# A decoder layer on one Trainium2 core: scores of query blocks 4 and 5 in three PSUM banks a head instead of four

## The chip, the cores and the metric

The kernel runs on one core of a Trainium2 chip. Its time is the device time of one execution, in microseconds (us). A core has five engines that run side by side, each through its own list of instructions: TensorE (PE in the profile) multiplies matrices, VectorE (DVE), ScalarE (ACT) and GpSimd (POOL) work on elements, SyncE (SP) issues transfers. TensorE writes its products into PSUM, which has eight banks of 512 float32 columns on each of 128 partitions; VectorE and ScalarE read them there. A bank can be written again only when the last reader of what it held is done.

## The reference: what is computed

One layer of a decoder: 1024 tokens, width 1024, float32. The part that matters here is the sparse attention (8 heads of width 64 in 2 groups of 4, in blocks of 128 queries). For each query block and head it makes three softmaxes: over the selected keys, over a local window of 512 keys, and over 63 compressed keys. With 16 blocks of 64 keys to choose of 16, all keys up to the query are selected.

```
ss = jnp.einsum('qghd,gqkd->qghk', qi, k_sel) * scale     # selected keys
p_s = softmax(where(smask, ss, NEG))
sw = jnp.einsum('qghd,kgd->qghk', qi, k_win) * scale      # local keys
p_w = softmax(where(wmask, sw, NEG))
o = gi[..., 0:1] * o_c + gi[..., 1:2] * o_s + gi[..., 2:3] * o_w
```

Besides there are a retention mixer, projections, gates for both mixers and an MLP.

## The kernel before

Every float32 product is made of three fast products of operands that were split into a high and a low half (in the attention scores, of two). The kernel goes through the layer in stages; the change touches the attention stage alone, which the trace shows from 365 us to about 758 us.

**Units.** The attention stage is cut into 32 units: query blocks 7 down to 0, two key groups, two pairs of heads (line 1093). Unit n has a generator of scores, `scores` (line 962), and one of weighted sums, `pv` (line 1029). A third generator makes the gates of the mixers, `gate_pieces` (line 899), in pieces of eight steps of three matmuls; it has nothing to do with attention and fills TensorE in between.

**Order.** The order of TensorE's instructions is written out by hand (line 113). `place` (line 1097) gives each step of each generator a place on a line of time on which a unit has length 1: the steps of unit n's scores lie evenly between n - 1 + 0.08 and n - 1 + 0.6, so beside the weighted sums of unit n - 1 (constants on lines 41 and 42); the steps of pv of unit n lie between n and n + 1.05; the gates take 8 steps a unit there. `prep_q` (line 948), which transposes the queries of the next group, lies at 0.9 before every second unit. The sorted list is then run step by step. How many steps the scores have, so how far they lie apart, says `n_scores` (line 1082). For the other engines the framework settles the order when the program is built.

**A step of scores.** A step takes a bank of the pool `psS` (four banks, line 937), makes two matmuls in it (tile `S`: high and low half of the queries), and then VectorE reduces each part of it (line 1007: it adds the mask, scales by -1/8 and takes the least value of each row, in place). When all parts of one softmax are reduced, VectorE takes the lesser of the two row values (line 1012), and ScalarE makes the exponentials (line 1016), which read the bank and write `pS` or `pW` in SBUF, with the sum of each row. The exponentials are the last readers of the bank. After the last ones of a head VectorE makes the factor `cf` (lines 1020 to 1023), and GpSimd scales `pS` and `pW` by it (line 1025).

**Banks of blocks 5 and 4.** Block 5 has 768 selected keys and 640 local ones, block 4 640 and 640. So a head has four steps and four banks: 512 selected keys; the other 256 (128) selected ones; 512 local keys; the last 128 local keys with the 64 compressed ones, which lie behind them in the key tile and are multiplied in the same two matmuls. The exponentials of the selected keys come after the second step, those of the local and the compressed keys after the fourth. A unit has two heads, so eight steps.

**A step of pv.** Weighted sums need the transpose of the probabilities. A step either transposes four blocks of 128 x 128 (lines 1060 and 1061) into a bank of the pool `psT` (two banks, line 938; tile `pt`), after which ScalarE copies the high half (`ph`, line 1062) and VectorE the low half (`pl`, line 1063), or it multiplies a pair that is two steps older by the values (tile `O`). The bank of `psT` is free when `pl` is done. `prep_q` takes its bank from the same two (tiles `QQ` on line 954 and `ql` on line 955). In block 5 a unit transposes six times; with T for transposing and M for multiplying the steps are T T T M T M T M T M M, and M again in the next unit.

**The gates' banks.** A piece of the gates holds one bank, of the pool `psO`, or, for odd pieces from number 15 on (line 907), one of `psS` for a whole unit; with four banks in that pool the scores of unit 14 (block 4) have three.

Of the kernel before, what the change touches and what calls it, by code (L numbers as in the profile page):

```python
# [9 lines left out]
F32 = mybir.dt.float32  # L10
F32R = mybir.dt.float32r
I32 = mybir.dt.int32
AF = mybir.ActivationFunctionType
OP = mybir.AluOpType
# [3 lines left out]
P = 128  # L18
S = 1024
# [5 lines left out]
BIGPOS = 3e38  # L25
# [84 lines left out]
def hybrid_block(ctx: ExitStack, tc: tile.TileContext, a: dict, out: bass.AP):  # L110
    nc = tc.nc
    V, A, G, T = nc.vector, nc.scalar, nc.gpsimd, nc.tensor
# [42 lines left out]
    def mm(o, w, m, start, stop):  # L155
        T.matmul(o, w, m, start=start, stop=stop)  # L156
# [60 lines left out]
    with ExitStack() as es:  # L217
# [12 lines left out]
        with ExitStack() as e1:  # L230
# [380 lines left out]
            tail = []  # L611
            for c in range(2):
                for j in range(NT if c else 0):
                    if j == NT - 1:
                        later(1, lambda: rt.update(t=ret_t(0)))
                    ps = psA.tile([P, 512], F32, name="mm", tag="mm")
# [318 lines left out]
    with ExitStack() as e3:  # L935
# [12 lines left out]
        def prep_q(qb, g):  # L948
# [10 lines left out]
                load_q(7 - nxt // 2, nxt % 2)  # L959
            yield  # L960

        def scores(qb, g, hp, u):
            QQ, ql = qs[qb, g]
            nk, nw = qb + 1, min(qb + 1, 5)
            cS, cW = nk * P, nw * P
            w0 = (nk - nw) * P
            u.update(nk=nk, nw=nw, P=[])

            def mask(c0, n, width, edge):
                if c0 + n == width:  # L970
                    return edge_m[:, 640 - n:]
                return edge_m[:, :n] if edge else edge_m[:, P:P + 1].to_broadcast([P, n])

            for i in range(2):
                h = hp * 2 + i
                sums = smp.tile([P, 5], F32, name="sums")
                mx = at.tile([P, 5], F32, name="mx", bufs=4)
                cf = at.tile([P, 3], F32, name="cf", bufs=4)
                pS = at.tile([P, 1024], F32, name="pS", bufs=PS_S)
                pW = at.tile([P, 768], F32, name="pW", bufs=PS_S)  # L980
                G.memset(pW[:, 704:], 0.0)
                for base, KK, start, width, p in ((1, KKs, 0, cS, pS), (2, KKw, w0, cW, pW)):
                    groups = []
                    for c0 in range(0, width, 512):
                        n = min(512, width - c0)
                        groups.append([(base if c0 == 0 else base + 2, KK, start + c0, n,
                                        mask(c0, n, width, base == 2), p[:, c0:c0 + n])])
                    split = len(groups) > 1
                    if base == 2:
                        tail = (0, KKc, 0, 64, cmp_m[:, 56 - 8 * qb:120 - 8 * qb], pW[:, 640:704])  # L990
                        if groups[-1][0][3] <= 448:
                            groups[-1].append(tail)
                        else:
                            groups.append([tail])
                    exps = []
                    for gi, grp in enumerate(groups):
                        ps = psS.tile([P, 512], F32, name="S")
                        off = 0
                        done = []
                        for b, K, c0, n, mk, o in grp:  # L1000
                            done.append((b, ps[:, off:off + n], mk, o))
                            off += n
                        _, K, c0 = grp[0][:3]
                        mm(ps[:, :off], QQ[:, h], K[:, g, c0:c0 + off], True, False)
                        mm(ps[:, :off], ql[:, h], K[:, g, c0:c0 + off], False, True)
                        for b, sc, mk, o in done:
                            V.tensor_tensor_reduce(sc, sc, mk, -0.125, BIGPOS, OP.add, OP.min, mx[:, b:b + 1])  # L1007
                            exps.append((b, sc, o))
                        if gi < len(groups) - 1:
                            yield  # L1010
                    if split:
                        V.tensor_tensor(mx[:, base:base + 1], mx[:, base:base + 1], mx[:, base + 2:base + 3],
                                        op=OP.min)
                    for b, sc, o in exps:
                        m = b - 2 if b > 2 else b
                        A.activation(o, sc, AF.Exp, bias=mx[:, m:m + 1], scale=-1.0, accum_out=sums[:, b:b + 1])  # L1016
                    if base == 1:
                        yield
                if cS > 512:
                    V.tensor_add(sums[:, 1:3], sums[:, 1:3], sums[:, 3:5])  # L1020
                V.reciprocal(cf, sums[:, :3])
                hd = g * 4 + hp * 2 + i
                V.tensor_mul(cf, cf, gts[:, qb, hd * 3:hd * 3 + 3])
                for b, v in ((1, pS[:, :cS]), (2, pW[:, :cW]), (0, pW[:, 640:704])):
                    G.tensor_scalar(v, v, cf[:, b:b + 1], 1.0, op0=OP.mult, op1=OP.mult)  # L1025
                u["P"].append((pS, pW))
                yield
# [53 lines left out]

        def n_scores(qb):
            sel, win = (qb + 4) // 4, (min(qb + 1, 5) + 3) // 4 + (1 if qb == 3 else 0)
            return 2 * (sel + win)

        def n_pv(qb):
            return 2 * ((qb + 1 + min(qb + 1, 5) + 2) // 2)
# [608 lines left out]
```

## Time and profile before

| | |
|---|---|
| time, median of 3 runs | 1570.58 us (1570.36 to 1570.7) |
| the profiled execution's own time | 1570.09 us |
| its span, first to last instruction | 1568.3 us |
| mean granted TensorE clock | 0.999 |
| matmuls shown / instructions | 7845 / 22711 |
| scores of units 8 to 15 (blocks 5 and 4) | about 505 to 606 us |

In the profile a line of the timeline has the start in us, the duration, the engine, the line of the kernel (L1016 is line 1016), the operation, the tiles as output<-inputs, and in brackets the time for which the engine was idle before it with what ended that. L156 is the helper `mm` of all matmuls, so there the tile tells what it is: `S` scores, `O` weighted sums, `gps` gates, `pt` transposes. PEld is the load of the fixed operand, which goes on beside the matmuls. The ends of matmuls are modelled, so the distance from one start to the next says what a matmul costs, not its duration.

### The profile page before, as it was taken

The numbers are of one execution on the slowest core, as the hardware profiler recorded it, in microseconds if no ns is written. First come the engines' busy times: TensorE is split into PE (matmuls) and PEld (weight loads), VectorE is DVE, ScalarE is ACT, GpSimd is POOL, SyncE is SP. The second block draws the span as 40 slices with busy tenths as digits, with TensorE's granted clock in tenths as the row PEclk, the third lists the DMA queues.
The fourth block names the chain that finished last, engine by engine and source line by source line (L and its number), as shares of the span: only waits on it lengthen the run. The fifth ranks groups of instructions, "written<-read, shape, count | busy, mean of one in ns | idle before, by whom it ended". The sixth has DMA issues, their size and how long they took to land.

```text
span 1568.3 us, 22711 instructions
## 1 busy us (share of the span) xinstructions
PE 1544.0 (98%) x7845; PEld 1293.8 (82%) x7845; DVE 1084.4 (69%) x2213; ACT 729.2 (46%) x1633; POOL 418.5 (27%) x496
## 2 busy tenths in 40 slices
PE   9999999999999999999999999999999999999997
PEld 7788888987888888888888888788888888888886
DVE  6875664765777777776755379777777677876673
ACT  5653553754676767676522134222222244443452
POOL 3020010001333323333000001654444446521320
PEclk9999999999999999999999999999999999999999
DMA  6202111342111111121544332544444597664472
GB/s 226 68 18 64 58 32 27 113 150 77 48 35 55 41 42 55 48 61 61 181 155 150 109 119 95 165 168 151 149 156 157 185 379 243 210 211 129 144 272 88
DMA packets 99157, 191.85 MB, mean 122 GB/s; under 512 B 26633, under 2 KB 30097, under 8 KB 99041
## 3 DMA queue, kind: packets, MB, share of 16 engines
q1 hardware_dynamic: 97584, 186.87, 36.2%
q10 hardware_dynamic: 832, 1.64, 0.3%
q0 software_dynamic: 624, 1.88, 0.3%
q8 instruction: 62, 1.02, 0.3%
q14 instruction: 55, 0.44, 0.1%
HBM read 140.02 MB, written 50.33 MB: 121 GB/s over the span
## 4 chain that ended last, share of the span: by engine, by line
PE 86%; DVE 6%; ACT 3%; issue 2%; POOL 1%; POOLq 0%; ACTq 0%; DVEq 0%
PE mmu L156 23%; PE mm L156 20%; PE mmd L156 19%; PE gps L156 9%; PE S L156 4%; PE O L156 3%; PE pt L1061 2%; PE pt L1060 2%; ACT pW L1016 1%; PE pO L156 1%; DVE S L1007 1%; DVE pl L1063 1%; PE pc L156 1%; ACT pS L1016 1%; PE pD L156 0%
## 5 line engine op out<-in xcount | busy, mean ns | idle before, releaser
L1213 DVE TENSOR_TENSOR wl<-raw,wh 128x1024 fp32r<-128x1024 f32 x121 | 185.2, 1556 | 65.5 <-ACT wh L1212 64.0
L1212 ACT ACTIVATE wh<-raw 128x1024 fp32r<-128x1024 f32 x121 | 125.4, 1056 | 207.7 <-PE mmd L156 125.7
L156 PE MATMUL mmd<-wh 128*128 128x512 f32 x448 | 174.3, 389 | 0.0
L156 PE MATMUL mmd<-wl,wh 128*128 128x512 f32 x448 | 174.3, 389 | 0.0
L156 PE MATMUL mmd<-wh,wl 128*128 128x512 f32 x448 | 174.3, 389 | 0.0
L156 PE MATMUL mm<-wh,bh 128*128 128x512 f32 (+1 forms) x416 | 160.8, 390 | 1.6 <-ACT bh L269 1.3
L156 PE MATMUL mm<-wh,bl 128*128 128x512 f32 (+1 forms) x416 | 154.9, 376 | 0.0
L156 PE MATMUL mm<-wl,bh 128*128 128x512 f32 (+1 forms) x416 | 154.3, 375 | 0.0
L1063 DVE TENSOR_TENSOR pl<-pt,ph 128x512 fp32r<-128x512 f32 (+1 forms) x160 | 103.8, 649 | 32.1 <-ACT ph L1062 29.8
L1062 ACT ACTIVATE ph<-pt 128x512 fp32r<-128x512 f32 (+1 forms) x160 | 90.5, 568 | 55.2 <-PE pt L1061 52.8
L1007 DVE CUSTOM_DVE_ANT_0 S<-S,edge_m 128x512 f32<-128x512 f32 (+3 forms) x192 | 100.9, 530 | 16.4 <-PE S L156 14.0
L156 PE MATMUL gps<-bh,wh 128*128 128x512 f32 x256 | 108.3, 423 | 1.2 <-ACT gst L919 1.2
L1025 POOL TENSOR_SCALAR pS<-pS,cf 128x1024 f32<-128x1024 f32 (+7 forms) x64 | 47.8, 747 | 229.8 <-ACT ph L1062 62.6
L1294 POOL TENSOR_TENSOR sf<-raw 128x512 f32<-128x512 f32 x14 | 22.7, 1622 | 295.8 <-DVE wl L1213 290.8
L156 PE MATMUL gps<-bh,wl 128*128 128x512 f32 x256 | 100.6, 393 | 0.0
L156 PE MATMUL gps<-bl,wh 128*128 128x512 f32 x256 | 100.5, 393 | 0.0
L156 PE MATMUL mmu<-bh,wh 128*128 128x512 f32 x256 | 99.7, 389 | 0.0
L156 PE MATMUL mmu<-bh,wl 128*128 128x512 f32 x256 | 99.6, 389 | 0.0
L156 PE MATMUL mmu<-bl,wh 128*128 128x512 f32 x256 | 99.6, 389 | 0.0
L156 PEld LDWEIGHTS mmd<-wh,wl 128*128 128x128 f32 x448 | 84.1, 188 | 17.6
L156 PEld LDWEIGHTS mmd<-wh 128*128 128x128 f32 x448 | 84.1, 188 | 17.5
L156 PEld LDWEIGHTS mmd<-wl,wh 128*128 128x128 f32 x448 | 84.1, 188 | 17.3
(362 smaller groups left out, 4042.3 us busy)
## 6 DMA issues: line engine op xcount, KB each, us to landing
raw<-u_scr SPq DMA_DIRECT2D x56, 512.0 KB, 4.0
raw<-w_down SPq DMA_DIRECT2D x41, 512.0 KB, 5.0
raw<-w_up SPq DMA_DIRECT2D x32, 512.0 KB, 3.6
u_scr<-u SPq DMA_DIRECT2D x60, 256.0 KB, 2.2
u_scr<-s SPq DMA_DIRECT2D x45, 256.0 KB, 2.0
y<-w_down SPq DMA_DIRECT2D x14, 512.0 KB, 7.8
x<-x SPq DMA_DIRECT2D x8, 512.0 KB, 5.7
qt<-q_scr SPq DMA_DIRECT2D x32, 128.0 KB, 2.4
```

Of the source, the lines that this page charges most:

```text
L156: T.matmul(o, w, m, start=start, stop=stop)
L1007: V.tensor_tensor_reduce(sc, sc, mk, -0.125, BIGPOS, OP.add, OP.min, mx[:, b:b + 1])
L1016: A.activation(o, sc, AF.Exp, bias=mx[:, m:m + 1], scale=-1.0, accum_out=sums[:, b:b + 1])
L1025: G.tensor_scalar(v, v, cf[:, b:b + 1], 1.0, op0=OP.mult, op1=OP.mult)
L1060: T.transpose(tp[:, bi * 2], p0, ident)
L1061: T.transpose(tp[:, bi * 2 + 1], p1, ident)
L1062: A.activation(ph[:, :n], tp[:, :n], AF.Copy)
L1063: V.tensor_sub(pl[:, :n], tp[:, :n], ph[:, :n])
L1212: A.activation(h[:, :n], r, AF.Copy)
L1213: V.tensor_sub(l[:, :n], r, h[:, :n])
L1294: eng.tensor_tensor(F[:, 1], x11, x21, op=OP.subtract)
```

## The change

Blocks 4 and 5 get three steps and three banks a head. The second bank takes the other selected keys, the last 128 local keys and the 64 compressed ones side by side (448 columns in block 5, 320 in block 4), with two pairs of matmuls: one pair for the selected keys, one for the 192 others. Then come its three reductions, one after the other, the lesser value for the selected keys, and the exponentials of the selected keys (both parts) and of the compressed ones. The third bank takes the first 512 local keys; after its reduction come the exponentials of all local keys, those in the second bank among them. The matmuls, reductions and exponentials are as many and as large as before. `n_scores` gives six steps a unit instead of eight, so the same stretch of 0.52 unit is cut into six parts. For the other blocks the rewritten loop makes the same instructions in the same order.

In the list of steps unit 9, with the weighted sums of unit 8 (sc: scores; T, M: pv; g: gates; q: `prep_q`), goes so:

```
before: g sc0 T sc1 g T sc2 sc3 g M sc4 T sc5 g sc6 M g sc7 T g M T g q M g M
after:  g sc0 T g sc1 T sc2 g M sc3 T g sc4 M sc5 g T g M T g q M g M
```

```diff
                 load_q(7 - nxt // 2, nxt % 2)
             yield
 
+        def packed(qb):
+            return qb in (4, 5)
+
         def scores(qb, g, hp, u):
             QQ, ql = qs[qb, g]
             nk, nw = qb + 1, min(qb + 1, 5)
@@ -979,42 +982,48 @@
                 pS = at.tile([P, 1024], F32, name="pS", bufs=PS_S)
                 pW = at.tile([P, 768], F32, name="pW", bufs=PS_S)
                 G.memset(pW[:, 704:], 0.0)
+                parts = {}
                 for base, KK, start, width, p in ((1, KKs, 0, cS, pS), (2, KKw, w0, cW, pW)):
-                    groups = []
-                    for c0 in range(0, width, 512):
-                        n = min(512, width - c0)
-                        groups.append([(base if c0 == 0 else base + 2, KK, start + c0, n,
-                                        mask(c0, n, width, base == 2), p[:, c0:c0 + n])])
-                    split = len(groups) > 1
-                    if base == 2:
-                        tail = (0, KKc, 0, 64, cmp_m[:, 56 - 8 * qb:120 - 8 * qb], pW[:, 640:704])
-                        if groups[-1][0][3] <= 448:
-                            groups[-1].append(tail)
+                    parts[base] = [(base if c0 == 0 else base + 2, KK, start + c0, min(512, width - c0),
+                                    mask(c0, min(512, width - c0), width, base == 2), p[:, c0:min(width, c0 + 512)])
+                                   for c0 in range(0, width, 512)]
+                tail = (0, KKc, 0, 64, cmp_m[:, 56 - 8 * qb:120 - 8 * qb], pW[:, 640:704])
+                if packed(qb):
+                    groups = [parts[1][:1], parts[1][1:] + parts[2][1:] + [tail], parts[2][:1]]
+                    ready = [(), (1, 0), (2,)]
+                else:
+                    groups = [[v] for v in parts[1] + parts[2]]
+                    if groups[-1][0][3] <= 448:
+                        groups[-1].append(tail)
+                    else:
+                        groups.append([tail])
+                    ready = [()] * len(groups)
+                    ready[len(parts[1]) - 1] = (1,)
+                    ready[-1] = (2, 0)
+                exps = {0: [], 1: [], 2: []}
+                for grp, rdy in zip(groups, ready):
+                    ps = psS.tile([P, 512], F32, name="S")
+                    off, runs, done = 0, [], []
+                    for b, K, c0, n, mk, o in grp:
+                        done.append((b, ps[:, off:off + n], mk, o))
+                        if K is KKc and runs:
+                            runs[-1][3] += n
                         else:
-                            groups.append([tail])
-                    exps = []
-                    for gi, grp in enumerate(groups):
-                        ps = psS.tile([P, 512], F32, name="S")
-                        off = 0
-                        done = []
-                        for b, K, c0, n, mk, o in grp:
-                            done.append((b, ps[:, off:off + n], mk, o))
-                            off += n
-                        _, K, c0 = grp[0][:3]
-                        mm(ps[:, :off], QQ[:, h], K[:, g, c0:c0 + off], True, False)
-                        mm(ps[:, :off], ql[:, h], K[:, g, c0:c0 + off], False, True)
-                        for b, sc, mk, o in done:
-                            V.tensor_tensor_reduce(sc, sc, mk, -0.125, BIGPOS, OP.add, OP.min, mx[:, b:b + 1])
-                            exps.append((b, sc, o))
-                        if gi < len(groups) - 1:
-                            yield
-                    if split:
-                        V.tensor_tensor(mx[:, base:base + 1], mx[:, base:base + 1], mx[:, base + 2:base + 3],
-                                        op=OP.min)
-                    for b, sc, o in exps:
-                        m = b - 2 if b > 2 else b
-                        A.activation(o, sc, AF.Exp, bias=mx[:, m:m + 1], scale=-1.0, accum_out=sums[:, b:b + 1])
-                    if base == 1:
+                            runs.append([K, c0, off, n])
+                        off += n
+                    for K, c0, o0, n in runs:
+                        mm(ps[:, o0:o0 + n], QQ[:, h], K[:, g, c0:c0 + n], True, False)
+                        mm(ps[:, o0:o0 + n], ql[:, h], K[:, g, c0:c0 + n], False, True)
+                    for b, sc, mk, o in done:
+                        V.tensor_tensor_reduce(sc, sc, mk, -0.125, BIGPOS, OP.add, OP.min, mx[:, b:b + 1])
+                        exps[b - 2 if b > 2 else b].append((b, sc, o))
+                    for m in rdy:
+                        if len(exps[m]) > 1:
+                            V.tensor_tensor(mx[:, m:m + 1], mx[:, m:m + 1], mx[:, m + 2:m + 3], op=OP.min)
+                    for m in rdy:
+                        for b, sc, o in sorted(exps[m], key=lambda v: v[0]):
+                            A.activation(o, sc, AF.Exp, bias=mx[:, m:m + 1], scale=-1.0, accum_out=sums[:, b:b + 1])
+                    if grp is not groups[-1]:
                         yield
                 if cS > 512:
                     V.tensor_add(sums[:, 1:3], sums[:, 1:3], sums[:, 3:5])
@@ -1081,7 +1090,7 @@
 
         def n_scores(qb):
             sel, win = (qb + 4) // 4, (min(qb + 1, 5) + 3) // 4 + (1 if qb == 3 else 0)
-            return 2 * (sel + win)
+            return 2 * (3 if packed(qb) else sel + win)
 
         def n_pv(qb):
             return 2 * ((qb + 1 + min(qb + 1, 5) + 2) // 2)
```

## The prediction

> **What bounds the kernel now.** I read the page first, then the waits of TensorE, then the stretches in which the scores of blocks 5 and 4 are made, then one of them instruction by instruction.
>
> ```profile
> span 1568.3 us, 22711 instructions
> PE 1544.0 (98%) x7845; PEld 1293.8 (82%) x7845; DVE 1084.4 (69%) x2213; ACT 729.2 (46%) x1633; POOL 418.5 (27%) x496
> ```
>
> TensorE is busy all the time, and the change takes no matmul away. So all that can be won is idle time of TensorE, and all that can be lost is new idle time. The waits of TensorE from 505.15 to 619 us, which holds all eight units, are one row:
>
> ```profile
> PE S L156 <- ACT pS L1016: 2.1, 4, 0.9
> ```
>
> It waits there four times, 2.1 us, always before a score matmul, always for an exponential: for a bank. A wait costs more than it shows:
>
> ```profile
> 509.83 0.28 PE L156 MATMUL O<-ph,Vs 128*128 128x256 f32 x1
> 510.48 0.50 PE L156 MATMUL S<-KKs,QQ 128*128 128x512 f32 x1 [0.37 <-ACT pS L1016]
> 510.82 0.39 PE L156 MATMUL S<-KKs,ql 128*128 128x512 f32 x1
> 581.16 0.36 PE L156 MATMUL S<-KKw,QQ 128*128 128x192 f32 x1 [0.89 <-ACT pS L1016]
> 586.70 0.36 PE L156 MATMUL S<-KKw,QQ 128*128 128x192 f32 x1 [0.45 <-ACT pS L1016]
> 505.84 0.39 PE L156 MATMUL S<-KKs,QQ 128*128 128x512 f32 x1
> 506.06 0.39 PE L156 MATMUL S<-KKs,ql 128*128 128x512 f32 x1
> 506.30 0.27 PE L1060 MATMUL pt<-ident,pS 128*128 128x128 f32 x1
> ```
>
> Undisturbed, a 512-column pair takes 0.46 us (505.84 to 506.30), 0.22 for its first half; after the wait of 0.37 the first half took 0.34. The step before is over some 0.12 after 509.83. So that wait cost 0.53 + 0.12 = 0.65, its 0.37 and 0.28. Four such are 2.1 + 4 x 0.28 = 3.2 us. The two at 581.16 and 586.70 lie in the unit whose gates hold a fourth bank: 0.89 + 0.45 + 0.56 = 1.9 of the 3.2.
>
> The engines that free the banks have little room there:
>
> ```profile
> 505.15:562.87 57.72, 56.97 (x362) 48.96 (x360) 44.66 (x157) 41.02 (x118) 18.95 (x34) 1.00 0.15 47
> ```
>
> The columns after the length are PE, PEld, DVE, ACT and POOL: VectorE is busy 44.66 of 57.72 us (77%), ScalarE 41.02 (71%). These averages hide runs. The exponentials of the first head of unit 9 are such a run:
>
> ```profile
> 509.65 0.69 ACT L1016 ACTIVATE pS<-S,mx 128x512 f32<-128x512 f32 x1 [0.74 <-DVE mx L1012]
> 512.15 0.60 ACT L1062 ACTIVATE ph<-pt 128x512 fp32r<-128x512 f32 x1
> ```
>
> From 509.65 to 512.15 five of them run without a gap: 2.50 us. The copy `ph` that follows waits for all of them. The second head is different:
>
> ```profile
> 513.49 0.47 ACT L1016 ACTIVATE pS<-S,mx 128x256 f32<-128x256 f32 x1
> 514.93 0.60 ACT L1062 ACTIVATE ph<-pt 128x512 fp32r<-128x512 f32 x1 [0.88 <-PE pt L1061]
> 515.42 0.68 ACT L1016 ACTIVATE pW<-S,mx 128x512 f32<-128x512 f32 x1
> 516.08 0.37 ACT L1016 ACTIVATE pW<-S,mx 128x128 f32<-128x128 f32 x1
> 516.43 0.32 ACT L1016 ACTIVATE pW<-S,mx 128x64 f32<-128x64 f32 x1
> 516.72 0.61 ACT L1062 ACTIVATE ph<-pt 128x512 fp32r<-128x512 f32 x1
> ```
>
> Two steps lie between its second and fourth bank, so its exponentials come in two runs, and `ph` at 514.93 gets in between. At 516.08 and 516.43 ScalarE takes exponentials that are earlier in the program before a `ph` that is later.
>
> **What the change does, part by part.** Counts and sizes stay: matmuls, reductions, exponentials, copies, DMA issues and their queues cost nothing new. What changes is when a bank is asked for and when the exponentials are ready.
>
> *First, the banks.* With three a head, the second head's first bank is the spare one, its second takes the bank of the first head's first part, its third that of the third part. I lay out unit 9 anew. From the transposes at 514.23 on, the order of TensorE's steps is as before, so I keep its clock there and count backwards:
>
> ```profile
> 514.03 0.25 PE L156 MATMUL S<-KKw,QQ 128*128 128x192 f32 x1
> 514.23 0.27 PE L1060 MATMUL pt<-ident,pW 128*128 128x128 f32 x1
> 514.59 0.48 PE L156 MATMUL gps<-bh,wh 128*128 128x512 f32 x1
> 515.36 0.28 PE L156 MATMUL O<-pl,Vs 128*64 128x256 f32 x1
> 515.84 0.27 PE L1060 MATMUL pt<-ident,pW 128*128 128x128 f32 x1
> 516.98 0.60 PE L951 MATMUL pt<-ident,qt 128*128 128x128 f32 x4
> 517.88 0.40 PE L156 MATMUL gps<-bh,wh 128*128 128x512 f32 x1
> 518.57 0.28 PE L156 MATMUL O<-pl,Vw 128*64 128x256 f32 x1
> 519.05 0.27 PE L1060 MATMUL pt<-ident,pS 128*128 128x128 f32 x1
> 506.65 0.36 PE L156 MATMUL S<-KKs,QQ 128*128 128x256 f32 x1
> 506.97 0.39 PE L156 MATMUL gps<-bh,wh 128*128 128x512 f32 x1
> ```
>
> A step of gates takes 0.69 (517.88 to 518.57), multiplying 0.48, transposing 0.36 and 0.08 on the step behind it. The shared bank takes 0.32 (506.65 to 506.97) and 0.20 (514.03 to 514.23). Backwards: gates from 513.54, third bank from 513.08, multiplying from 512.60, shared bank from 512.08 to 512.60, gates from 511.31, transposing 510.87, first bank from 510.41. The first head's third bank is then made some 1.6 before that (gates and multiplying, 1.17, and its own 0.46), at 508.8, and its shared bank at 507.8 to 508.35. Its exponentials can start some 1.7 after that, at 510.1 (1.45 as worked out below, and some delay by a `pl`), and end 2.5 later: the first part's bank is free near 511.0, wanted at 512.08, and the third part's near 512.3, wanted at 513.08. So the waits with four banks go; spare are 0.8 to 1.1 us. With three (unit 14) the second head's first bank must wait for the first part's: wanted 510.41, free 511.0, 0.6 left. Gain 3.2 - 0.6 = 2.6 us.
>
> *Second, the exponentials of the second head.* They now hang on three reductions in a row:
>
> ```profile
> 512.03 0.43 DVE L1007 CUSTOM_DVE_ANT_0 S<-S,edge_m 128x256 f32<-128x256 f32 x1
> 514.43 0.30 DVE L1007 CUSTOM_DVE_ANT_0 S<-S,edge_m 128x128 f32<-128x128 f32 x1
> 514.83 0.23 DVE L1007 CUSTOM_DVE_ANT_0 S<-S,cmp_m 128x64 f32<-128x64 f32 x1
> 514.98 0.23 DVE L1012 TENSOR_TENSOR mx<-mx 128x1 f32<-128x1 f32 x1
> 517.14 0.16 DVE L1023 TENSOR_TENSOR cf<-cf,gts 128x3 f32<-128x3 f32 x1
> 517.36 0.69 DVE L1063 TENSOR_TENSOR pl<-pt,ph 128x512 fp32r<-128x512 f32 x1
> 517.47 0.91 POOL L1025 TENSOR_SCALAR pS<-pS,cf 128x768 f32<-128x768 f32 x1 [0.78 <-ACT ph L1062]
> ```
>
> The row at 514.43 starts 0.2 after the last matmul of its bank has been followed (514.23). So the three may start at 512.8 and take 0.5 + 0.40 + 0.15, the lesser value 0.1, then ScalarE 0.1: 514.05, if VectorE is free. It isn't: the factor of the first head, whose exponentials end at 512.6, takes some 0.5, and `pl` of the transposes at 510.87, whose `ph` waits for those exponentials too, 0.6. With the first alone the exponentials start at 514.55, with both at 515.15. I take 514.5.
>
> From there all five are ready in a row, as the last reduction (513.08 + 0.46 + its 0.7) is done by then or during the first three: 2.5 us, to 517.0. The transposes at 514.23 asked for their `ph` at 514.93; now it comes at 517.0, and `pl`, 0.64 later as at 516.72 and 517.36, ends at 518.35. `psT` has two banks; the transposes at 515.84 hold the other. `prep_q` wants one at 516.98 and gets it at 518.45: a new wait of 1.45 us. In units without `prep_q` everything behind it comes 0.44 earlier (its own 0.36 and 0.08); the multiplying that needs this `pl` is then at 518.13 and waits 0.4. There are four of each: 4 x 1.45 + 4 x 0.4 = 7.4. In block 4 a 256-wide exponential and reduction are 128 wide (0.37 for 0.47, 0.30 for 0.43); with GpSimd's smaller part I take 0.3 off in each of four units, 1.2.
>
> **Sum:** 7.4 - 1.2 - 2.6 = +3.6 us, nothing after it hides that: the rest of the kernel is TensorE's too (98%). The profiled execution's own time, 1570.09, becomes 1573.7; the median of the runs, 1570.58, is 0.49 above it, so 1574.2.
>
> If VectorE has more to do, the start slips past 514.93 and `ph` gets in first; the exponentials then run 515.45 to 517.95. `prep_q` is served, but the factor follows the last exponential by 0.75 up to GpSimd's start (516.72 to 517.47), the scaling takes 0.91: 519.7 with 0.1 to start, and the next unit's transposes want it at 519.05 (518.6 without `prep_q`). Waits of 0.65 and 1.1, again 7.0, less 1.2 and 2.6: +3.2. Bounds of this case: start at 514.1, 0.4 less in all eight but never below nothing, 4 x 1.05: +0.4; start at 514.9, just ahead of `ph`: 4 x 1.85 + 4 x 0.8 = 10.6, +6.8.
>
> [...]
>
> **Rivals.** *Banks only, faster.* Only the waits for banks go: -3.2 to -2.6 us, 1567.4 to 1568.0. It decides if the five exponentials start before 514.3 and `ph` still gets in among them: then they end by 517.3, GpSimd is done by 519.05 (0.75 + 0.91 + 0.1), and nothing is late. For it: VectorE is idle for 23%, and all four waits are for banks. Against: 514.05 is the earliest start that I can build, and it needs a VectorE without its other work. [...]
>
> *Even.* `ph` gets in among the exponentials, as at 514.93 now, because the third bank's reduction comes behind a `pl`, but they start as late as forecast. `prep_q` isn't held, the run ends 0.5 later, and half of the eight units wait some 0.65 for GpSimd: 2.6, against 2.6 won: 1570.6, within 0.8.
>
> *The bank's wait only moves.* The shared bank is held until the second run. If ScalarE is 1 us later than laid out, the second head's third bank waits too, 0.3 a unit: 2.4 us more, 1576.6; I count it in the upper end.
>
> **How the numbers follow.** Forecast (a wait for `ph`, `pl` or GpSimd at the end of each unit) 0.62; banks only 0.19; even 0.19. Its own range is 1571.0 to 1577.4 (+0.4 to +6.8). 0.2% is 3.1 us, about what a measurement of this kernel tells from no change: slower than that is some two thirds of the forecast with the last rival in it and a little of the even case, 0.44; faster is half of the banks-only case, whose ends lie on both sides of it, 0.1; the rest, 0.46. The range reaches down into banks only, to 1567.5.
>
> **What would show it.** In the profile after: no row S <- ACT in the waits from 505 to 580 us, one near 0.6 us in unit 14; at the end of units 9, 11, 13 and 15 five exponentials in a row with no `ph` between, and a wait of `pt` L951 for `pl`, 1 to 1.9 us each; 0.3 to 1.1 us in the others, for `pl` or for `pS` L1025. The prediction is wrong if `ph` runs between exponentials of the second head and TensorE's waits in this stretch are under 2 us in all.

## The result and the profile after

The changed kernel takes 1579.84 us (median of 4 runs, 1577.57 to 1581.59), the kernel before, measured together with it, 1570.6: a ratio of 1.0057, 95% interval 1.0045 to 1.0069. That is 9.2 us slower, two and a half times the 3.6 forecast, and above the range. The direction was right, the size was not.

The execution that was profiled took 1577.57 us, with a span of 1575.8 (before 1570.09 and 1568.3). So the trace explains 7.5 us; another 2.3 lie between this execution and the median. Both parts have to be found.

The page of the changed kernel shows as many instructions on each of the five engines and nearly the same busy times as before:

```profile
span 1575.8 us, 22678 instructions
PE 1544.4 (98%) x7845; PEld 1293.8 (82%) x7845; DVE 1088.6 (69%) x2213; ACT 728.9 (46%) x1633; POOL 417.9 (27%) x496
```

The work is the same; the 7.5 us are idle time of TensorE. Its waits from 500 to 622 us (what waited, for what, us in total, times, longest):

```profile
PE pt L951 <- DVE pl L1072: 7.8, 4, 2.1
PE O L156 <- DVE pl L1072: 1.8, 3, 0.9
PE pt L1070 <- POOL pS L1034: 0.4, 1, 0.4
```

Before, the same view had 2.1 us of waits for a bank and one of 0.4 for `pS`. The waits for a bank are gone, all of them, in unit 14 too. In their place stand four waits of the queries' transposes (L951) of 2 us each and three of a multiplying, all for `pl`. 10.0 us against 2.5: this is the 7.5.

This stretch holds the scores of units 9 to 15. Those of unit 8, the first of block 5, lie ahead of it: in the kernel before, its score matmuls start from 490.96 to 499.06, so the 505 us given for the start of the eight units above, and the window of the prediction, leave it out. That changes no sum: from 470 to 506 us neither kernel waits for a bank, only for `pS` (1.0 us before, 0.9 after).

How one of them comes about, in unit 9. First ScalarE, then VectorE, then TensorE (start, length, engine, line, operation):

```profile
512.40 0.60 ACT L1071 ACTIVATE ph<-pt 128x512 fp32r<-128x512 f32 x1
515.13 0.69 ACT L1025 ACTIVATE pS<-S,mx 128x512 f32<-128x512 f32 x1 [2.14 <-DVE mx L1022]
...
517.40 0.38 ACT L1025 ACTIVATE pW<-S,mx 128x128 f32<-128x128 f32 x1
517.65 0.22 ACT L1025 ACTIVATION_READ_ACCUMULATOR pW<-S,mx 128x1 f32 x1
517.74 1.10 ACT L1071 ACTIVATE ph<-pt 128x512 fp32r<-128x512 f32 x2
```

```profile
513.09 0.69 DVE L1072 TENSOR_TENSOR pl<-pt,ph 128x512 fp32r<-128x512 f32 x1
513.69 0.42 DVE L1018 CUSTOM_DVE_ANT_0 S<-S,edge_m 128x256 f32<-128x256 f32 x1
514.03 0.14 DVE L1018 DVE_READ_ACCUMULATOR2_ANT mx<- 128x1 f32 x1
514.21 0.30 DVE L1018 CUSTOM_DVE_ANT_0 S<-S,edge_m 128x128 f32<-128x128 f32 x1
514.42 0.14 DVE L1018 DVE_READ_ACCUMULATOR2_ANT mx<- 128x1 f32 x1
514.42 0.61 DVE L1022 TENSOR_TENSOR mx<-mx 128x1 f32<-128x1 f32 x1
...
518.45 1.28 DVE L1072 TENSOR_TENSOR pl<-pt,ph 128x512 fp32r<-128x512 f32 x2
```

```profile
514.56 0.27 PE L1070 MATMUL pt<-ident,pW 128*128 128x128 f32 x1
...
516.75 0.39 PE L156 MATMUL gps<-bh,wl 128*128 128x512 f32 x1
519.19 0.66 PE L951 MATMUL pt<-ident,qt 128*128 128x128 f32 x4 [2.06 <-DVE pl L1072]
```

Read it backwards. The queries' transposes start at 519.19, after a wait of 2.06, when the first of two `pl` (from 518.45) has let their bank go. Both `ph` stood on ScalarE until 517.74, behind the five exponentials, which ran from 515.13. And ahead of these ScalarE was idle for 2.14 us. The last transpose of the first of the two `ph` starts at 514.56. Where a `ph` waits for nothing else it starts 0.37 us after that (505.82 after 505.45, 507.64 after 507.27), so this one was ready near 514.93. For the last 0.2 us of its pause ScalarE sat idle beside it, because the exponentials come first in its order; then it made all five. They were ready no earlier because VectorE did the first head's factor and the earlier `pl` (513.09) ahead of the second head's reductions (513.69 and 514.21), and the lesser value took 0.61 us.

### The profile page after: what moved, and what is told of

Read it like the earlier page. It is cut to its first block, busy times and chain, and to the rows that moved or that the text cites. A ratio compares the mean times of both kernels' runs of the same rounds, so it can differ in the third digit from the quotient of the medians.

```text
span 1575.8 us, 22678 instructions
## 1 busy us (share of the span) xinstructions
PE 1544.4 (98%) x7845; PEld 1293.8 (82%) x7845; DVE 1088.6 (69%) x2213; ACT 728.9 (46%) x1633; POOL 417.9 (27%) x496
## 4 chain that ended last, share of the span: by engine, by line
PE 83%; DVE 8%; ACT 4%; issue 2%; POOL 1%; DMA 0%; POOLq 0%; ACTq 0%; DVEq 0%
PE mmu L156 23%; PE mm L156 20%; PE mmd L156 19%; PE gps L156 8%; PE S L156 3%; PE O L156 3%; ACT pW L1025 2%; PE pt L1070 2%; PE pt L1069 1%; DVE pl L1072 1%; DVE S L1018 1%; PE pO L156 1%; PE pc L156 1%; ACT pS L1025 1%; ACT ph L1071 1%
## 5 line engine op out<-in xcount | busy, mean ns | idle before, releaser
L1222 DVE TENSOR_TENSOR wl<-raw,wh 128x1024 fp32r<-128x1024 f32 x121 | 188.6, 1584 | 64.7 <-ACT wh L1221 62.0
L1018 DVE CUSTOM_DVE_ANT_0 S<-S,edge_m 128x512 f32<-128x512 f32 (+3 forms) x192 | 101.5, 531 | 12.3 <-PE S L156 10.6
L1303 POOL TENSOR_TENSOR sf<-raw 128x512 f32<-128x512 f32 x14 | 22.7, 1624 | 295.6 <-DVE wl L1222 290.8
```

The source lines that it names most:

```text
L1222: V.tensor_sub(l[:, :n], r, h[:, :n])
L1303: eng.tensor_tensor(F[:, 1], x11, x21, op=OP.subtract)
```

## The experiments

Of each diff below the lines that matter are shown. Theory A: the time is lost because the joined exponentials stand ahead of a `ph` in ScalarE's fixed order; the `ph` is late, its `pl` holds a bank of the transposes' pool, and the queries' transposes wait. Rival B: the six wider-spaced steps cost the time, the waits only show it. Theory C stands beside either: TensorE's waits of 2 us lower its clock in some executions, which makes the other 2.3 us.

| run | us, median | before, measured with it | ratio (95%) | waits of TensorE, 500 to 622 us |
|---|---|---|---|---|
| the change | 1579.84 | 1570.6 | 1.0057 (1.0045-1.0069) | 10.0 |
| e0_again | 1580.75 | 1570.31 | 1.0065 (1.0053-1.0078) | 10.2 |
| e1_q_bank | 1571.62 | 1570.31 | 1.0009 (1.0000-1.0018) | 3.7 |
| e2_split | 1579.71 | 1570.31 | 1.0061 (1.0049-1.0074) | 10.6 |
| e3_old_places | 1575.65 | 1570.31 | 1.0034 (1.0022-1.0047) | 5.3 |
| e4_joined | 1572.53 | 1569.95 | 1.0014 (1.0005-1.0023) | 3.1 |
| e5_last_later | 1574.34 | 1569.95 | 1.0027 (1.0018-1.0037) | 6.6 |
| e6_last_later_q_bank | 1571.01 | 1569.95 | 1.0007 (0.9998-1.0015) | 3.8 |
| e7_one_unit | 1568.71 | 1569.95 | 0.9993 (0.9984-1.0002) | 1.6 |
| e10_ph_first | 1574.75 | 1570.28 | 1.0027 (1.0017-1.0037) | 5.3 |
| e11_one_unit_again | 1568.76 | 1570.28 | 0.9991 (0.9982-1.0000) | 1.7 |

The last column is the sum of the rows of the waits of that profile (before: 2.5). A wait cost more than it shows, 0.28 us in the rows of the prediction and 0.15 in those above (L951 starts at 519.19 instead of 516.98, 2.21 later, with a wait of 2.06), so many short ones weigh more here than their sum.

**Another bank for the queries (e1_q_bank).** Only the bank that was waited for changes; ScalarE's order is that of the changed kernel.

```diff
-            tp = psT.tile([P, 4, P], F32, name="pt", tag="pt")
+            if (qb, g) in ((5, 1), (4, 0), (4, 1), (3, 0)):
+                tp = psS.tile([P, 4, P], F32, name="pt", tag="S")
+            else:
+                tp = psT.tile([P, 4, P], F32, name="pt", tag="pt")
```

> The changed kernel, but in the four units of blocks 5 and 4 that prepare the next queries, the queries' transposes take a bank of the scores' pool instead of the transposes' pool. The order on ScalarE and VectorE stays that of the changed kernel. Theory A (the time is lost because the five exponentials of the second head run in one row, the copy ph behind them comes 2.6 us late, and the queries' transposes, L951, wait for the bank that pl still holds): the four waits of L951 for pl, 8.6 us in the profile of the changed kernel, go to under 1 us in all; the multiplying that needs the same pl or the next transposes that need GpSimd's scaled pS wait 0.5 to 1 us in these units instead, since the copies are still late; 1572.5 to 1574.5 us. Rival B (the wider spacing of six steps over the unit where eight were costs the time, and the waits of L951 are only where it shows): about as slow as the changed kernel, 1578 to 1580, with waits of the same sum under another line. Rival C (the changed kernel's runs differ by 4 us because long waits of TensorE lower its clock): the runs of this kernel lie within 1 us of each other, as the waits of 2 us are gone; without C they spread as those of the changed kernel.

```profile
PE O L156 <- DVE pl L1075: 3.4, 6, 0.9
PE pt L1073 <- POOL pS L1037: 0.3, 1, 0.3
```

1571.62 us: 9 us of the loss are gone with the four waits of L951, 0.9 us better than the lower end of what A expected. The `ph` is as late as ever (from 517.58 in unit 9); what waits for its `pl` now is the multiplying, 0.9 us at most. The steps stand at the six wide places, so B falls. Ten of the eleven runs lie within 1 us, the other at 1573.45.

**`ph` first (e10_ph_first).** The changed kernel with `ph` ahead of the second head's four large exponentials on ScalarE. For that the last step of scores stands 0.05 unit later, and these exponentials wait for one lesser value of both kinds of keys; the smallest exponential (64 wide) stays ahead of `ph`.

```diff
+                    if packed(qb) and i == 1:
+                        rdy = {2: (1, 2)}.get(rdy[0], (0,)) if rdy else ()
+                        if rdy == (1, 2):
+                            V.tensor_tensor(mx[:, 1:3], mx[:, 1:3], mx[:, 3:5], op=OP.min)
...
-                        if len(exps[m]) > 1:
+                        if len(exps[m]) > 1 and not (packed(qb) and i == 1):
...
-            place(scores(qb, g, hp, u), n_scores(qb), n - 1 + S_BEG, n - 1 + S_END)
+                    todo.append((n - 1 + S_BEG + w * (k + 0.5) + (0.05 if k == 5 else 0), len(todo), it))
```

> The changed kernel with its three banks a head and its places, but on ScalarE the copy ph of the transposes stands before the second head's exponentials instead of behind them. To get this order, these exponentials wait for one least-value instruction over both kinds of keys, 2 columns wide, and the last of the six steps stands 0.05 of a unit, 0.7 us, later. So the exponentials start later than in the changed kernel. Theory A (the queries' transposes wait because a ready ph stands behind exponentials that aren't ready in ScalarE's fixed order): the waits of L951 for pl go to under 0.3 us each although the exponentials are later; instead the next unit's first transposes wait for GpSimd's scaled pS, 0.3 to 1.3 us a unit; 1572 to 1577 us. Rival (the lateness of the exponentials itself holds L951): the waits of L951 stay near 2 us.

```profile
516.34 0.58 ACT L1075 ACTIVATE ph<-pt 128x512 fp32r<-128x512 f32 x1
516.82 0.69 ACT L1029 ACTIVATE pS<-S,mx 128x512 f32<-128x512 f32 x1
...
518.93 0.62 ACT L1075 ACTIVATE ph<-pt 128x512 fp32r<-128x512 f32 x1
```

```profile
PE pt L1074 <- POOL pS L1038: 4.8, 6, 1.7
PE pt L1073 <- DVE pl L1076: 0.5, 2, 0.2
```

The exponentials now run from 516.82 and end after 518.8. All of TensorE's steps stand 1.04 us later here than in the changed kernel (the gates' at 515.63 is there at 514.59), mainly by a wait of 1.68 at 506.22. Counted from these steps the exponentials start 0.65 us later than in the changed kernel and end 0.15 later, and the `ph` comes 2.4 earlier; and no transposes of queries wait at all. So it is the place of `ph` in the order and not the lateness of the exponentials that held them. What the lateness costs shows in the first row: GpSimd's scaling is late for the next unit. 1574.75 us, some 6 less than e0_again. Of what is left, 1.4 us lie outside this stage in the profiled execution: a single wait for `u`, late in the kernel, is 2.4 us long, where it is 1.0 before.

**The change once more (e0_again).** 

> The changed kernel once more, in the same company. Theory A: 1577 to 1581 us, four waits of the queries' transposes for pl of 1.9 to 2.3 us each. Rival C (the clock falls for some us in some executions because of these waits): the runs spread over 3 us or more, and an execution with a mean clock under 0.998 shows a clock of 0.5 or less in the stretch from 505 to 615 us; without C the clock is lower elsewhere, and the runs of the kernel before spread as much.

1580.75 us, with four waits of L951 of 1.74 to 2.45 us. The runs spread from 1577.82 to 1583.18, as theory C expected. This profile has a stretch at half clock; it is read with the runs on the clock.

**Splitting the run (e2_split).** The last two exponentials are issued behind the transposes.

```diff
+                    if packed(qb) and grp is groups[-1]:
+                        yield
                     for m in rdy:
...
+                    if k in (2, 5):
+                        todo.append((n - 1 + S_BEG + w * (k + 0.5) + 0.1, len(todo), it))
```

> The changed kernel, but the least value and the exponentials of the local keys of the second head are issued at a place of their own, one step later, behind the transposes that stood behind them. ScalarE's fixed order in block 5 (units 9 to 11) then has the copy ph before the last two exponentials; in block 4 a ph stands between these two. Nothing else moves. Theory A (ScalarE takes its instructions in the order in which the program was built, so a ph that is ready waits behind exponentials that are not): the waits of L951 in units 9 and 11 fall from 2.2 us to under 1 us each, in units 13 and 15 by some 1 us each; 1574 to 1576 us. Rival B (the wider spacing costs the time): no change in the sum of the waits, 1578 to 1580.

```profile
PE pt L1072 <- POOL pS L1036: 5.7, 4, 2.2
PE pt L951 <- DVE pl L1074: 4.9, 4, 1.4
```

A miss: 1574 to 1576 us were expected. L951 waits 4.9 us instead of 7.8, as the order predicts in part, but 1579.71 us is no gain: the last two exponentials now end behind a `ph`, GpSimd's scaling starts later, and the next unit's transposes wait 5.7 us for it. The expectation had left this end of the chain out. The three exponentials of the first part still stood ahead of the `ph` (at 516.77). Behind the longest of these waits, 2.19 us up to 567.08, this profile too shows half clock, 0.50 from 567.7 to 571.1.

**Places closer together (e3_old_places, e5_last_later, e6_last_later_q_bank).** The first gives the six steps the first six of the eight places of before, the second moves the last of these by one place, the third adds the other bank of e1_q_bank.

```diff
-            return 2 * (3 if packed(qb) else sel + win)
+            return 2 * (sel + win)
```
```diff
+                for k in (0, 1, 2, 3, 4, 6):
+                    todo.append((n - 1 + S_BEG + (S_END - S_BEG) * (k + 0.5) / 8, len(todo), it))
```

> The changed kernel with three banks a head, but its six steps stand at the first six of the eight places that the kernel before had, so that they are closer together and the second head is done two places earlier. The order of exponentials and ph on ScalarE stays as in the changed kernel. Theory A (the run of five exponentials starts too late for the ph behind it): the run starts 1 to 1.3 us earlier, the waits of L951 for pl fall from 2.1 to 0.8 to 1.2 us each, and some waits for a bank come back, 0.3 to 0.6 us in a few units, as steps are closer; 1574 to 1577 us. Rival B (the wider spacing alone costs the time): all of the loss goes, 1569 to 1571.

> The changed kernel with its six steps at the first five and the seventh of the eight places of before: the first five as in the run with the old places, the last one place, 0.94 us, later, which gives the bank that it reuses as much longer. Theory A (both ends of one chain: steps that come early wait for a bank, steps that come late end the exponentials late): the waits for a bank before third parts go, those in the unit with three banks stay at about 2.5 us, the waits of L951 for pl grow from 0.4 to about 1 us each; in all no better than the old places by more than 1.5 us, 1574 to 1576. Rival (the banks alone were what the old places lost): 1571 to 1573.

> The run before this one in the list, with the queries' transposes in a bank of the scores' pool. Theory A: the waits of L951 for pl go, and the multiplying that needs that pl waits 0.3 to 0.7 us in these units; what stays is the unit with three banks, 2.5 us, and some small ones; 1571.5 to 1573.5 us, not under the kernel before. Rival (banks alone): under 1570 us.

The waits of e3_old_places, but for one of 0.3 us:

```profile
PE S L156 <- ACT pW L1025: 3.1, 4, 1.2
PE S L156 <- ACT pS L1025: 1.3, 1, 1.3
PE pt L951 <- DVE pl L1072: 0.6, 2, 0.3
```

and the three largest rows of e5_last_later:

```profile
PE pt L951 <- DVE pl L1072: 2.7, 4, 0.9
PE S L156 <- ACT pW L1025: 1.8, 2, 1.2
PE S L156 <- ACT pS L1025: 1.0, 1, 1.0
```

With earlier steps the exponentials start at 513.46, L951 hardly waits (0.3 us at most, where 0.8 to 1.2 were expected), and the waits for a bank that the change removed are back and larger (4.4 us with three banks a head, 2.1 before with four). One place later, some of these go and L951 waits again. It is one chain with two ends: 1575.65 and 1574.34 us. With the other bank as well it is 1571.01. The waits of L951 are gone; of the 3.8 us left, 2.2 are two waits for a bank in unit 14, which three banks with steps so close can't serve, 0.5 one in unit 12, 0.7 one for a `pl` and 0.3 one for the gates.

**Joining alone (e4_joined).** The kernel before, with four banks and eight places; in four units the second head's exponentials wait for all four reductions.

```diff
+                    join = i == 1 and hp == 1 and qb in (4, 5)
+                    if join and base == 2:
+                        V.tensor_tensor(mx[:, 1:3], mx[:, 1:3], mx[:, 3:5], op=OP.min)
+                        exps = held + exps
+                    elif join:
+                        held, exps = exps, []
```

> The kernel before, with its four banks a head and eight places, but in the four units that prepare the next queries the second head's exponentials are joined: one least-value instruction for both kinds of keys, 2 columns wide, behind the fourth bank's reduction, so that all five exponentials wait for all four banks. No bank is shared. Theory A (joining the second head's exponentials costs the time, whatever the banks do): the run of five starts near 515.5 and ends near 518 us in unit 9; on ScalarE the ph at 514.9 now comes before it, so the queries' transposes wait little, but the factor and GpSimd's scaling end near 519.8, 0.7 to 1.3 us after the next unit's first transposes want them; four waits of that size in these units, 1573 to 1575 us. Rival B (the six places instead of eight, or the shared bank, cost the time): no new waits, 1570 to 1571 us.

```profile
515.22 0.60 ACT L1069 ACTIVATE ph<-pt 128x512 fp32r<-128x512 f32 x1 [2.17 <-PE pt L1068]
515.71 0.69 ACT L1023 ACTIVATE pS<-S,mx 128x512 f32<-128x512 f32 x1
```

The exponentials run from 515.71, behind the `ph`, and L951 doesn't wait. At the head of the next units TensorE loses 0.4, 0.4, 0.8 and 0.5 us against the kernel before (by the starts of the gates' steps); the waits listed there, for `pl` and for GpSimd, are 0.15 to 0.24, well under the 0.7 to 1.3 expected. It is 2.6 us slower (ratio 1.0005 to 1.0023), under the expected 3 to 5. Joining costs by itself, but little as long as the `ph` stands ahead.

**Waits put in on purpose (e8_waits_short, e9_waits_long).** The kernel before, with 16 waits in the last projections, 1 copy or 3 copies long.

```diff
+                    if off == 0:
+                        src = pp[0]
+                        for _ in range(3):
+                            hold = tmp.tile([P, 512], F32R, name="hold")
+                            A.activation(hold, src, AF.Copy)
+                            src = hold
+                        mm(ps[:, :64], hold[:, :P], hold[:, :64], True, True)
```

> The kernel before with 16 waits of TensorE put into a later stage, two for each of the eight column blocks of the last projections: ahead of the second product stands a small matmul on a copy that ScalarE makes of the first product. The copy's values are not used in the output. One copy: a wait of about 1 us (0.6 for the copy and some 0.4 to notice and start). Rival C (waits of about 2 us lower TensorE's clock, waits of 1 us don't): no stretch of half clock between 780 and 1560 us; 16 x 1.1 us longer, some 1588 us. Without C (the half clock of 3.41 us seen in two profiles had another cause): the same here as with long waits.

> The same 16 waits, but three copies one after the other ahead of the small matmul: a wait of about 2.3 us each, as long as those of the queries' transposes in the changed kernel. Rival C: several stretches of half clock of 3.41 us, each just behind a wait, in a quarter to three quarters of the 16; each costs up to 1.7 us beside its wait; some 1610 to 1625 us. Without C: none, 1570 + 16 x 2.4 = 1608 us.

The waits came to 0.75 us (14 of them; the first two 1.72 and 1.47) and 2.07 (14; the first two 2.85 and 3.37). The stretches of the two kernels that hold nearly all of them; the third figure from the right is the mean granted clock:

```profile
780.00:1000.00 220.00, 208.75 (x938) 168.19 (x939) 127.75 (x183) 66.46 (x113) 3.14 (x2) 1.00 0.36 117
```
```profile
780.00:920.00 140.00, 109.00 (x400) 84.24 (x401) 53.11 (x72) 47.33 (x72) 0.00 (x0) 0.88 0.29 91
815.80:819.20 3.40, 1.33 (x7) 0.82 (x6) 1.28 (x2) 1.85 (x3) 0.00 (x0) 1.00 0.49 154
819.20:822.60 3.40, 3.40 (x9) 2.63 (x9) 0.00 (x0) 0.00 (x0) 0.00 (x0) 0.50 0.02 5
```

With 0.75 us the clock stays at 1.00. (At 772.66, behind the one wait of 1.72, it is halved for 3.41 us.) With 2.07 us it is 0.88 over 140 us: at half clock for 140 x 0.12 / 0.5 = 33.6 us, some ten times 3.41, behind 10 of the 16 waits. The two last rows are one of them: 1.33 us of work in 3.4 us, then half clock in the next 3.4. The kernel with short waits takes 1592.99 us (2 runs), 22.7 more than before, with 13.6 us of waits; without the one halving, taken as 1.4, that leaves 7.7 / 16 = 0.48 around each. That with long waits takes 1627.71 (2 runs), 57.4 more: 35.2 of waits, 7.7 around them, and 14.5 for ten halvings, 1.45 us each; the two profiled executions alone (1592.55 and 1628.59 us) give 1.6. Both kernels took longer than expected (1588 and 1610 to 1625), and the half clock came where theory C has it: behind waits of 2 us, not behind those of 0.75.

**The change in one unit (e7_one_unit, e11_one_unit_again).** Unit 14 alone, where before waits 0.89 and 0.45 us.

```diff
-        def packed(qb):
-            return qb in (4, 5)
+        def packed(qb, g, hp):
+            return (qb, g, hp) == (4, 1, 0)
```

> The change in one unit of the eight alone: the scores of the first two heads of block 4's second group, the unit whose gates hold a fourth bank and in which the kernel before waits 0.89 and 0.45 us for a bank; the other seven units as before. It prepares no queries. Theory A (the change pays where a bank is waited for and no queries are prepared): these two waits, 1.7 us with what they delay, go, and one wait of 0.3 to 0.7 us for pl comes; 1.0 to 1.4 us less than before, 1569.0 to 1569.6, about a third of what can be told from no change. Rival B (the spacing costs about 1 us in each unit): 1570.3 or more.

> The change in one unit alone once more, for a narrower interval: 1.0 to 1.4 us less than the kernel before, by the two waits of that unit that go and the one wait for pl that comes.

The waits of e11_one_unit_again; in e7_one_unit the last row is 0.4, the others are the same:

```profile
PE S L156 <- ACT pS L1025: 0.7, 2, 0.4
PE O L156 <- DVE pl L1072: 0.5, 1, 0.5
PE pt L1070 <- POOL pS L1034: 0.5, 1, 0.5
```

1568.71 and 1568.76 us, 1.2 and 1.5 under the kernel before, measured with each. Both intervals reach 1, so neither alone tells it from no change; the trace has the two waits of that unit gone and one of 0.5 for `pl` come, as expected (the other two rows are there before too). It has the shortest time of the study, and it is the one place where the waits that the change removes outweigh those that it brings.

## Why the prediction missed

**The banks: right.** All four waits were to go but for 0.6 us in unit 14. They went, that rest too: 3.2 us won instead of 2.6.

**The exponentials of the second head: the mechanism right.** Five in a row, 2.6 us against 2.5 forecast, the `ph` behind them, `pl` late, L951 waiting in four units and the multiplying in others: every link is in the trace, and e1_q_bank and e10_ph_first each break it at one link and lose these waits.

**The step that failed** is the start of this run, and what was to follow if it slipped: "If VectorE has more to do, the start slips past 514.93 and `ph` gets in first". The working had both values: 514.55 if VectorE does the factor alone first, 515.15 with `pl` too. It did both, and the start was 515.13; I took 514.5. That 515.15 fits so closely is luck: only two of the three reductions stood ahead (0.73 us, for 1.05 with three), but the lesser value took 0.61, for 0.1.

The later start was then let off by a rule that doesn't hold in this trace: ScalarE didn't take what was ready first. Its order was fixed when the program was built, exponentials ahead of `ph`. In unit 9 `ph` was ready near 514.93, and ScalarE, idle until 515.13, passed it over for the exponentials; the same, for 0.2 to 0.3 us, in units 10, 11 and 15. (In units 12 to 14 the exponentials had begun up to 0.1 us before `ph` was ready.) I had the right row (at 516.08 and 516.43 ScalarE takes exponentials ahead of a `ph`) and read it as an order of the program, but then used readiness for the alternative. The `ph` of unit 9, ready near 514.93, ran at 517.74, behind all five exponentials. Worked through with 515.15 and no way past, the run ends at 517.65, `pl` at 519.0, and L951 starts 2.1 us late; it started 2.21 late.

So the terms, with what each wait delays. L951: 8.5 us instead of 5.8 (2.22 and 2.25 in block 5, 1.93 and 2.10 in block 4). The multiplying: 2.3 instead of 1.6, in three of the four units (1.05 in block 5, 0.55 and 0.68 in block 4; unit 8's didn't wait). The credit of 1.2 for block 4 is within these figures, some 0.2 us for each L951 and 0.4 for each multiplying, about as taken. The banks: 3.2 won instead of 2.6. 8.5 + 2.3 - 3.2 = 7.6 us, against 7.5 in the span. The upper bound, a start just ahead of `ph`, was taken as the worst case; without the let-off it isn't one.

**What the sum had no term for** is the clock. In the profiled execution it is 1.00 throughout the stretch. In that of e0_again, 1579.25 us, one wait of 1.93 us is followed by half clock. Two of its waits, each with the 3.4 us that hold it and the next:

```profile
607.60:611.00 3.40, 1.47 (x10) 0.99 (x10) 1.66 (x8) 2.52 (x12) 1.04 (x4) 1.00 0.00 0
611.00:614.40 3.40, 3.40 (x16) 3.00 (x14) 0.69 (x1) 1.19 (x2) 1.06 (x2) 0.50 0.26 60
```
```profile
515.40:518.80 3.40, 1.51 (x11) 1.04 (x9) 1.27 (x9) 3.33 (x12) 0.34 (x3) 1.00 0.00 0
518.80:522.20 3.40, 2.84 (x22) 2.66 (x23) 1.80 (x3) 1.41 (x4) 1.97 (x3) 1.00 0.27 61
```

In e9_waits_long, whether a wait was followed by half clock hung on where it fell on a grid of periods of 3.41 us (worked out below). The grid's place differs between profiled executions: a half clock starts at 567.7 us in e2_split, 781.63 in e9_waits_long and 1569.24, at the very end, in the change, 62.7 and 230.7 periods apart. In the profiled execution of the change, with the grid counted back from 1569.24 at the 3.4135 us of e9_waits_long, the longest pieces of the four waits within one period come to 1.31, 1.86, 1.33 and 1.39 us, each to some 0.1 (0.0003 us a period, over some 300 periods), an estimate that takes the grid to run on unbroken; none is followed by half clock. In e0_again they are 1.91, 1.08, 1.22 and 1.93, and only the last is.

Four waits of 2 us an execution, each with some chance of a halving that costs about 1.45: the runs of the change lie at 1577.57, 1579.09, 1580.6 and 1581.59, with mean clocks of 0.998, 0.998, 0.997 and 0.996. None, one, two and about three halvings would give 1577.6, 1579.0, 1580.5 and 1581.9. That the median's 2.3 us are this is inferred: e9_waits_long shows it for such waits, and the profile of e0_again shows one halving in this kernel; the other executions weren't profiled.

**The rivals.** *Banks only* came true in one unit (e7_one_unit), where no queries are prepared. *Even* and *the bank's wait only moves* fell: `ph` didn't get in, and no bank was waited for; the latter is what closer places bring (e3_old_places).

## What to carry to other kernels

When work is joined, ask what stands behind it in the fixed order of its engine, ready or not: ScalarE, which took its instructions in order here, idled 0.2 us beside ready work in unit 9, so a late start was paid in full by all that followed (L951 2.21 us late). If two starts come out of the working, go on with both to the end, and let neither off by another order without looking at how the order is made. A wait of TensorE cost its length, some 0.15 (the change) to 0.5 us (e8_waits_short) around it and, where 1.7 us or more of it fell into one period of 3.41 us, in most cases some 1.5 us of half clock behind it.

## What the runs showed of the hardware

All ten halvings of e9_waits_long start on one grid of 3.41 us, whatever the waits' own places: 781.63, 791.87, 802.11, 819.18 and so on to 907.93, always whole multiples apart; from the first to the last it is 126.30 us, 37 times 3.4135. What counted there was how much of a wait fell into one period: of the 14 waits of 2.07 us the nine that were followed by half clock had 1.86 us or more within one, the other five were cut by the grid with 1.56 at most on one side. The first two waits, 2.85 and 3.37 long, agree: the one, cut into 1.43 and 1.42, has none; the other, with 2.96 in one period, has. The rows of e0_again are near the edge: 1.47 us of work in 3.4 and half clock behind it, 1.51 and none. Two periods of e9_waits_long with some 1.55 of work did lose the clock, and the one of e8_waits_short with 1.69, so the edge isn't one number of this measure; that stays open. Pieces of 1.72 us (e8_waits_short), 1.86 or more (e9_waits_long) and 1.93 (e0_again) within one period were followed by half clock, though about 1.86 (the change) and 1.91 (e0_again) were not.

The lesser value of the selected keys' two columns took 0.61 to 0.64 us for the second head of seven units (9 to 15) in the changed kernel, against a median of 0.16 over all 30 of these instructions in this stretch. In unit 9 that is 0.46 us of the start. That it stands right behind its reductions isn't the reason: the first heads' stand behind the same two and took 0.15 or 0.16. The cause stays open.
